# Seven block products of a SwiGLU pair in another order, in turn between two PSUM banks, and another tile for a pair's first weights

## The chip, the cores and the metric

The kernel runs on one core of one Trainium2 chip, in one launch. The metric is the device time of that core in microseconds, the median of several runs. Besides the runs there is one profiled execution with its own time.

## What is computed

Two layers of a decoder trunk on 256 positions of 1024 channels, in float32. Each layer is a half-step SwiGLU FFN, a token mixing, a second half-step SwiGLU FFN, each followed by a layer normalisation of the residual:

```python
def swiglu(x, wg, wu, wd):
    return (jax.nn.silu(x @ wg) * (x @ wu)) @ wd

def reference(x, ...):
    for l in range(DEPTH):                                   # DEPTH = 2
        x = layer_norm(ALPHA * x + 0.5 * swiglu(x, ffn_wg[l, 0], ffn_wu[l, 0], ffn_wd[l, 0]), ln_g[l, 0], ln_b[l, 0])
        m = token_mix(x, w_in[l], w_out[l], ...)
        x = layer_norm(ALPHA * x + m, ln_g[l, 1], ln_b[l, 1])
        x = layer_norm(ALPHA * x + 0.5 * swiglu(x, ffn_wg[l, 1], ffn_wu[l, 1], ffn_wd[l, 1]), ln_g[l, 2], ln_b[l, 2])
    return x
```

The FFN has 2816 hidden channels: `wg` and `wu` are 1024 x 2816, `wd` is 2816 x 1024. The token mixing (sparse attention, a pooling mixer, a gated linear attention, one input and one output projection) is not touched by the change.

## The kernel before

**Three matmuls for one.** The 256 positions are two tiles of 128 (t = 0, 1). A float32 product is made of three matmuls on values split in a high and a low part: high x high, high x low, low x high. ScalarE writes the high part of a weight block (`ACT.activation`, L232, L240, L260, L178: 128 x 1024 in about 1.05 us), VectorE the rest (`tensor_sub`, L233, L241, L262, L179: about 1.2 us for 1024 columns, 2.3 us for 2048). One *unit* of weights is two raw loads of 512 KB on SyncE's queue, split into one high tile `wh` and one low tile `wl` of 128 x 2048; there are four of each, and a unit's pair of tiles comes free when TensorE is done with it.

**Chunks and pairs.** The hidden channels are 11 chunks of 256. Chunks 0, 1 and 10 are computed plainly (`glu`, quarters of a chunk as units; `a10` and `b10` in the plan are the halves of chunk 10). Chunks 2 to 9 go in four pairs (2,3), (4,5), (6,7), (8,9), each by a Strassen-like scheme (Winograd's form) over two position tiles, two halves of the 1024 channels and the two chunks: seven block products in place of eight. `product` (L453) issues the 12 matmuls of one, of 512 columns each, at L462. Four of the seven use sums of the two position tiles (`make_sums`, named `sa` and `sb` in the trace), three use `xh`, `xl` themselves.

**Seven's weights** (`seven`, L134). Product 1 takes block 11 as it is; 5 takes 11 + 12; 6 takes 11 + 12 + 22; 4 takes 11 + 12 + 22 + 21 as the signs of the stored blocks make it; 7 takes 12 + 22, which a DMA on GpSimd's queue adds in place (L157); 3 takes 22, 2 takes 21. The running sum is built in the tile `fa`, into which block 11 is loaded (L142); VectorE adds 12, then 22 (L147), then 21 (L171), and each sum is split. `fa` shares its memory with the attention's keys, `fb` (block 12) with a weight of the mixing, `fc` (22) with a transposed tile of the attention. Block 21 goes into two of the four `raw` buffers that all plain units use.

**Banks.** Each pair holds two of four PSUM banks (named `g` and `tr` in the trace): `b1` and `b5`. Products 1, 6, 7 and 4 add up in `b1`; 5, and then 3 and 2, in `b5`:

```python
self.product(b1 if x in "1674" else b5, left[x], x in "15")
```

After a product its bank is copied out by ScalarE (`copy`, L476): 1 gives `c11`, 5 gives `cv`, 6, 7 and 3 the partial results of the second chunk. After 3 the copy `c11` is written into `b5` (L517) for product 2 to add to. `gated` (L527) applies SiLU and the product with the other half, on ScalarE and VectorE. The results are transposed by `h_T` (T in the plan) and split, and `down` (d in the plan, a unit of 24 matmuls, 12 for each position tile) multiplies them with `wd` into four banks `acc`.

**Order.** TensorE's order in this stage is written out by hand in `PLAN` and kept as written; S2, S4, S6, S8 open a pair. The units of weights are made in the same order, three units ahead of the one in use (`ahead`, L566). The other engines and queues are ordered by a scheduler that knows priorities: the copies and gates have a high one, but each engine works through its queue in order.

**Normalisation.** `ln_params` (L373) loads the 1024 scales and 1024 offsets to all 128 partitions, in two tiles, on GpSimd's queue, for the first normalisation on SyncE's; `layer_norm` (L385) uses them on VectorE (L400, L402) at the end of each of the six sub-layers.

Of the kernel before, what the change touches and what calls it, by code (L numbers as in the profile page):

```python
# [10 lines left out]
def _warn_once_fixed(msg, *args, **kwargs):  # L11
# [7 lines left out]
F32 = mybir.dt.float32  # L19
# [3 lines left out]
AF = mybir.ActivationFunctionType  # L23
# [4 lines left out]
D = 1024  # L28
# [9 lines left out]

PLAN = ("S2 1 T0 5 a10 6 b10 7 d0 3 4 2 S4 1 T2 d1 5 6 7 d2 3 4 2 S6 d3 1 T4 5 6 7 d4 3 4 2 "
        "S8 d5 1 T6 5 6 7 d6 T10 3 4 2 d7 T8").split()

LAST = (10, 8, 9)
WARM = ((7, 512), (4, 128))
# [11 lines left out]
def build(ctx, tc, d):  # L57
    nc = tc.nc
    PE, ACT, DVE, POOL = nc.tensor, nc.scalar, nc.vector, nc.gpsimd

    cst = ctx.enter_context(tc.tile_pool(name="cst", bufs=1))
    wp = ctx.enter_context(tc.tile_pool(name="wp", bufs=1))
    act = ctx.enter_context(tc.tile_pool(name="act", bufs=1))
# [53 lines left out]
    for t in range(2):  # L117
        vbd.append(cst.tile([128, 2, 2, 64], F32, name=f"vbd{t}"))
        a = cst.tile([128, 4, 128], F32, name=f"at{t}")
# [11 lines left out]
    def gate_up(l, f, c, q):  # L131
        return [d["wgu"][l, f, c, 2 * q + h] for h in range(2)]

    def seven(l, f, c):  # L134


        b = {}

        def load(to, c, q, pool, name, tag):
            b[to] = pool.tile([128, 2048], F32, name=name, tag=tag, bufs=1)  # L140
            for h, a in enumerate(gate_up(l, f, c, q)):
                last_dma[0] = nc.sync.dma_start(out=b[to][:, h * 1024:(h + 1) * 1024], in_=a)  # L142

        def add(x):
            for h in range(2):
                s = slice(h * 1024, (h + 1) * 1024)
                DVE.tensor_add(out=b["11"][:, s], in0=b["11"][:, s], in1=x[:, s])  # L147

        def f1():
            load("11", c, 0, cst, "fa", "ks")  # L150
            return split_wide(b["11"])

        def f5():
            load("12", c + 1, 0, cst, "fb", "s_w1")
            add(b["12"])
            for h, a in enumerate(gate_up(l, f, c + 1, 1)):
                nc.gpsimd.dma_start(out=b["12"][:, h * 1024:(h + 1) * 1024], in_=a, accum_op=ALU.add)  # L157
            return split_both(b["11"])

        def f6():  # L160
            load("22", c + 1, 1, mix, "fc", "pT")
            add(b["22"])
            return split_both(b["11"])

        def f4():
            b["21"] = []
            for h, a in enumerate(gate_up(l, f, c, 1)):
                raw = wp.tile([128, 1024], F32, name="raw", bufs=4)
                last_dma[0] = nc.sync.dma_start(out=raw, in_=a)
                s = slice(h * 1024, (h + 1) * 1024)  # L170
                DVE.tensor_add(out=b["11"][:, s], in0=b["11"][:, s], in1=raw)  # L171
                b["21"].append(raw)
            return split_both(b["11"])

        def f2():
            u = split_tiles()
            for raw, (wh, wl) in zip(b["21"], u):
                ACT.activation(out=wh, in_=raw, func=AF.Copy)  # L178
                DVE.tensor_sub(out=wl, in0=raw, in1=wh.bitcast(F32))  # L179
            return u  # L180

        return {"1": f1, "5": f5, "6": f6, "7": lambda: split_wide(b["12"]), "3": lambda: split_wide(b["22"]),
                "4": f4, "2": f2}

# [32 lines left out]
    last_dma = [None]  # L217
# [7 lines left out]
    def split_tiles():  # L225
        return in_halves(wide_tiles())
# [9 lines left out]
    def split_both(raw):  # L236
        u = split_tiles()
        for h, (wh, wl) in enumerate(u):
            s = slice(h * 1024, (h + 1) * 1024)
            ACT.activation(out=wh, in_=raw[:, s], func=AF.Copy)  # L240
            DVE.tensor_sub(out=wl, in0=raw[:, s], in1=wh.bitcast(F32))  # L241
        return u
# [109 lines left out]
    def make_sums(sums):  # L352

        s1, a11, a12, a21 = sums["s"], sums[0, 0], sums[0, 1], sums[1, 0]
        big = wp.tile([128, 2, 2, 4, 128], F32R, name="sb", tag="fb", bufs=1)

        def parts(f, i):
            tl = (mix.tile([128, 2, 4, 128], F32R, name=f"sa{i}", tag=("qs0", "qs1")[i], bufs=1) if i < 2
                  else big[:, i - 2])
            split(tl[:, 0], tl[:, 1], f.rearrange("p (a b) -> p a b", a=4))  # L360
            return tl[:, 0], tl[:, 1]
        first = parts(s1, 0)
        DVE.scalar_tensor_tensor(out=s1, in0=s1, scalar=-1.0, in1=a11, op0=ALU.mult, op1=ALU.subtract)
        DVE.tensor_sub(out=a21, in0=a11, in1=a21)
        DVE.scalar_tensor_tensor(out=a12, in0=a12, scalar=-1.0, in1=s1, op0=ALU.mult, op1=ALU.subtract)
        yield first
        yield parts(s1, 1)
        yield parts(a21, 2)
        yield parts(a12, 3)

    lnp = {}

    def ln_params(l, i):  # L373
        if (l, i) not in lnp:
            r = []
            for nm in ("ln_g", "ln_b"):
                tl = act.tile([128, D], F32, name="lnp_" + nm)
                src = d[nm][l, i]
                src = bass.AP(tensor=src.tensor, offset=src.offset, ap=[[0, 128], [1, D]])
                (nc.gpsimd if l + i else nc.sync).dma_start(out=tl, in_=src)  # L380
                r.append(tl)
            lnp[l, i] = r
        return lnp[l, i]

    def layer_norm(t, accs, l, i):  # L385
# [22 lines left out]
    class Ffn:  # L408
# [56 lines left out]
        def plan(self):  # L465
            a = [[tuple(p[:, 4 * q:4 * q + 4] for p in XT[t]) for q in range(2)] for t in range(2)]
            left = {"1": a[0][0], "2": a[0][1], "4": a[1][1]}
            sums = make_sums(self.sums)

            def f32():  # L470
                self.cc += 1
                return mix.tile([128, 512], F32, name="cc", tag=("vblk", "cc", "c40", "at011", "c41")[self.cc % 5], bufs=1)

            def copy(b, tag=None):
                r = mix.tile([128, 512], F32, name=tag, tag=tag, bufs=1) if tag else f32()
                ACT.activation(out=r, in_=b, func=AF.Copy)  # L476
                return r
            ahead_sums = [next(sums)]
            for x in PLAN:
                if x[0] == "S":  # L480
                    c = int(x[1:])

                    (w1, b1), (w5, b5) = self.bank(), self.bank()
                    if not m0 and c == 8:
                        with tc.issue_after(last_dma[0].ins):
                            late_constants()
                            m0.append(Mix(0))
                            ln_params(0, 0)
                elif x[0] in "abTd":
                    for t in range(2):  # L490
                        if x[0] == "T":
                            self.h_T(t, int(x[1:]) // 2)
                        elif x[0] == "d":
                            self.down(t, int(x[1:]))
                        else:
                            self.glu(t, int(x[1:]), "ab".index(x[0]))
                    continue
                else:
                    if x in "5673" and x not in left:
                        left[x] = ahead_sums.pop()  # L500
                        if x != "3":
                            ahead_sums.append(next(sums))
                    self.product(b1 if x in "1674" else b5, left[x], x in "15")
                with tc.high_priority():
                    if x == "1":
                        c11 = copy(b1)
                    elif x == "5":
                        v = copy(b5, "cv")
                    elif x == "6":
                        u = copy(b1)  # L510
                    elif x == "7":
                        c22 = copy(b1)
                        DVE.tensor_add(out=c22, in0=v, in1=c22)
                        self.gated(1, c + 1, c22, sign=-1.0)
                    elif x == "3":
                        w = copy(b5, "cw")
                        ACT.activation(out=b5, in_=c11, func=AF.Copy)  # L517
                        DVE.tensor_add(out=u, in0=w, in1=u)
                        self.gated(0, c + 1, u, sign=-1.0)
                    elif x == "2":  # L520
                        self.gated(0, c, b5, c11)
                        self.free.append(w5)
                    elif x == "4":
                        self.gated(1, c, b1, f32())
                        self.free.append(w1)
# [549 lines left out]
    for l in range(L):  # L1075
# [3 lines left out]
        out = [wout(m, t) for t in range(2)]  # L1079
# [104 lines left out]
```

## Time and profile before

| | |
|---|---|
| median of 3 runs | 1001.22 us (995.27 to 1007.08) |
| profiled execution, its own time | 999.5 us |
| its span, first to last instruction | 997.7 us |
| TensorE, matmuls / weight loads busy | 954.4 us (96%) / 773.8 us (78%) |
| VectorE, ScalarE, GpSimd busy | 850.5 us (85%), 637.6 us (64%), 56.3 us (6%) |
| HBM read | 193.68 MB, 195 GB/s over the span |
| mean granted clock of TensorE | 0.980 |

How to read the profile: a row of the timeline gives the start and the duration in us, the engine (PE is TensorE, DVE VectorE, ACT ScalarE, POOL GpSimd, SP SyncE; a "q" behind it is the engine's queue of issues), the source line, the operation, output<-inputs, shape, how many in a row, and in brackets how long the engine was idle before and what it waited for. Matmuls overlap: one of 512 columns is shown with a duration of 0.39 us, but the next may start earlier, so starts tell more than durations. A list of waits gives who waited for whom, us in total, how many times, and the longest. A table of windows gives for each stretch its length, the busy time and the count of each engine's instructions, the granted clock of TensorE, the DMA engines' share and GB/s.

### The profile page before, as it was taken

What the parts mean: (1) busy time and instruction counts of PE and PEld (TensorE: products, weight loads), DVE (VectorE), ACT (ScalarE), POOL (GpSimd) and SP (SyncE); (2) the same over time, 40 slices, a digit from 0 to 9 for tenths busy, and PEclk for the clock granted to TensorE, in tenths of its full rate; (3) what the DMA queues carried; (4) which work ended last, traced back from release to release, by engine and by line L of the source; (5) the groups of instructions that cost most, each with busy time, mean ns of one, the idle gap of its engine ahead of it and who ended that gap; (6) DMA issues with size and microseconds to landing.
All of it is one profiled execution on the core that took longest, in us unless ns stands there. A gap on an engine that the chain in (4) does not pass through costs nothing.

```text
span 997.7 us, 12731 instructions
## 1 busy us (share of the span) xinstructions
PE 954.4 (96%) x4579; PEld 773.8 (78%) x4579; DVE 850.5 (85%) x1194; ACT 637.6 (64%) x993; POOL 56.3 (6%) x82
## 2 busy tenths in 40 slices
PE   9989998999999999998999999899999999999997
PEld 6867786888778887877888877688887788877785
DVE  6978987787978979989799899887889699899884
ACT  6847657475675766667567667664677467677660
POOL 0000000010101000000000000001000010000000
PEclk9999998999999999999999999989999999999989
DMA  9856685665545575765857766565635366775551
GB/s 329 247 204 182 180 274 188 215 211 177 174 128 179 164 254 158 221 253 165 300 169 216 206 252 188 150 230 178 222 120 149 130 204 191 223 258 171 170 169 43
DMA packets 56480, 195.57 MB, mean 196 GB/s; under 512 B 7137, under 2 KB 8161, under 8 KB 56161
## 3 DMA queue, kind: packets, MB, share of 16 engines
q1 hardware_dynamic: 49824, 171.16, 49.9%
q0 software_dynamic: 6448, 23.53, 11.8%
q8 instruction: 36, 0.59, 0.2%
q14 instruction: 28, 0.22, 0.1%
q10 hardware_dynamic: 144, 0.07, 0.0%
HBM read 193.68 MB, written 1.05 MB: 195 GB/s over the span
## 4 chain that ended last, share of the span: by engine, by line
PE 56%; DVE 20%; ACT 8%; DMA 8%; issue 6%; POOL 0%; SPq 0%; DVEq 0%; POOLq 0%; ACTq 0%
PE acc L296 9%; PE acc L294 9%; PE acc L295 9%; PE tr L462 8%; DMA fa<-in_wgu 5%; PE g L462 5%; DVE wl L241 4%; DVE fa L147 4%; DVE wl L233 4%; ACT wh L232 3%; DMA fb<-in_wgu 2%; DVE wl L262 2%; PE tr L330 2%; ACT wh L260 2%; PE g L295 2%
## 5 line engine op out<-in xcount | busy, mean ns | idle before, releaser
L260 ACT ACTIVATE wh<-raw 128x1024 fp32r<-128x1024 f32 (+2 forms) x194 | 196.4, 1033 | 93.5 <-PE acc L296 44.6
L262 DVE TENSOR_TENSOR wl<-raw,wh 128x1024 fp32r<-128x1024 f32 (+2 forms) x194 | 226.3, 1188 | 20.3 <-ACT wh L260 19.8
L294 PE MATMUL acc<-wh,hi 128*128 128x512 f32 x352 | 138.5, 393 | 0.0
L295 PE MATMUL acc<-wl,hi 128*128 128x512 f32 x352 | 137.6, 391 | 0.0
L296 PE MATMUL acc<-wh,lo 128*128 128x512 f32 x352 | 137.3, 390 | 0.0
L240 ACT ACTIVATE wh<-fa 128x1024 fp32r<-128x1024 f32 x96 | 100.5, 1061 | 53.2 <-DVE fa L147 52.0
L241 DVE TENSOR_TENSOR wl<-fa,wh 128x1024 fp32r<-128x1024 f32 x96 | 115.7, 1221 | 2.1 <-ACT wh L240 1.6
L294 PEld LDWEIGHTS acc<-wh,hi 128*128 128x128 f32 x352 | 66.6, 189 | 13.6
L296 PEld LDWEIGHTS acc<-wh,lo 128*128 128x128 f32 x352 | 66.2, 188 | 14.0
L295 PEld LDWEIGHTS acc<-wl,hi 128*128 128x128 f32 x352 | 66.4, 189 | 13.6
L294 PE MATMUL acc<-wh,xh 128*128 128x512 f32 x192 | 76.3, 397 | 0.5 <-ACT xh L307 0.3
L296 PE MATMUL acc<-wh,xl 128*128 128x512 f32 x192 | 76.3, 397 | 0.0
L295 PE MATMUL acc<-wl,xh 128*128 128x512 f32 x192 | 76.0, 396 | 0.2 <-DVE wl L262 0.2
L462 PE MATMUL tr<-wh,sb 128*128 128x512 f32 x128 | 50.4, 459 | 14.3 <-ACT cc L476 14.3
L157 POOL DMA_DIRECT2D fb<-in_wgu x32 | 27.8, 870 | 492.3 <-DVE fa L147 300.9
L233 DVE TENSOR_TENSOR wl<-fa,wh 128x2048 fp32r<-128x2048 f32 x16 | 36.7, 2292 | 20.8 <-ACT wh L232 19.1
L462 PE MATMUL g<-wh,sb 128*128 128x512 f32 x128 | 43.6, 402 | 7.4 <-ACT cc L476 7.4
L462 PEld LDWEIGHTS tr<-wh,sb 128*128 128x128 f32 x128 | 28.5, 223 | 23.8 <-ACT cc L476 17.7
L232 ACT ACTIVATE wh<-fa 128x1024 fp32r<-128x1024 f32 x32 | 33.3, 1054 | 16.0 <-DMA fa<-in_wgu 10.4
L462 PE MATMUL g<-wh,sa 128*128 128x512 f32 x128 | 42.1, 395 | 0.0
L296 PEld LDWEIGHTS acc<-wh,xl 128*128 128x128 f32 x192 | 36.2, 188 | 7.6 <-DVE xl L308 0.6
L462 PE MATMUL tr<-wl,xh 128*128 128x512 f32 x96 | 38.5, 401 | 3.8 <-DVE wl L233 3.8
(288 smaller groups left out, 2191.9 us busy)
## 6 DMA issues: line engine op xcount, KB each, us to landing
raw<-in_wd SPq DMA_DIRECT2D x88, 512.0 KB, 5.1
raw<-in_wgu SPq DMA_DIRECT2D x79, 512.0 KB, 4.5
fa<-in_wgu SPq DMA_DIRECT2D x32, 512.0 KB, 5.1
fb<-in_wgu SPq DMA_DIRECT2D x32, 512.0 KB, 5.6
fc<-in_wgu SPq DMA_DIRECT2D x32, 512.0 KB, 5.7
fb<-in_wgu POOLq DMA_DIRECT2D x32, 512.0 KB, 6.8
raw<-in_win SPq DMA_DIRECT2D x32, 512.0 KB, 4.2
raw<-in_wout SPq DMA_DIRECT2D x16, 512.0 KB, 4.2
```

The source lines that it names most:

```text
L147: DVE.tensor_add(out=b["11"][:, s], in0=b["11"][:, s], in1=x[:, s])
L157: nc.gpsimd.dma_start(out=b["12"][:, h * 1024:(h + 1) * 1024], in_=a, accum_op=ALU.add)
L232: ACT.activation(out=wh[:, s], in_=raw[:, s], func=AF.Copy)
L233: DVE.tensor_sub(out=wl, in0=raw, in1=wh.bitcast(F32))
L240: ACT.activation(out=wh, in_=raw[:, s], func=AF.Copy)
L241: DVE.tensor_sub(out=wl, in0=raw[:, s], in1=wh.bitcast(F32))
L260: ACT.activation(out=wh[:, s], in_=raw[:, s], func=AF.Copy)
L262: DVE.tensor_sub(out=wl[:, s], in0=raw[:, s], in1=wh[:, s].bitcast(F32))
L294: pe(PE.matmul(ps, xh, wh, start=start, stop=False, skip_group_check=seeded))
L295: pe(PE.matmul(ps, xh, wl, start=False, stop=False, skip_group_check=seeded))
L296: pe(PE.matmul(ps, xl, wh, start=False, stop=stop, skip_group_check=seeded))
L462: pe(PE.matmul(ps, a[:, k, :], w[:, s], start=first and k == 0 and n == 0, stop=k == 3 and n == 2, skip_group_check=True))
```

## The change

The order of products in `PLAN` becomes 1 5 6 3 7 2 4, so that `b1` and `b5` follow each other in turn; the down units stand in other gaps between them. 2 now loads block 21 and 4 adds it later; `make_sums` gives its last two sums in the other order. Block 11 is loaded into a tile `fd` that shares its memory (tag `lnp`) with the normalisation's parameters, now one tile of 2 x 1024; 5's add reads `fd` and writes the running sum into `fa`. The parameters of the first normalisation are loaded on GpSimd's queue like the others.

```diff
-PLAN = ("S2 1 T0 5 a10 6 b10 7 d0 3 4 2 S4 1 T2 d1 5 6 7 d2 3 4 2 S6 d3 1 T4 5 6 7 d4 3 4 2 "
-        "S8 d5 1 T6 5 6 7 d6 T10 3 4 2 d7 T8").split()
+PLAN = ("S2 1 T0 5 a10 6 3 b10 7 2 d0 4 S4 1 T2 5 d1 6 3 d2 7 2 4 S6 d3 1 T4 5 6 d4 3 7 2 4 "
+        "S8 d5 1 T6 5 6 d6 3 T10 7 2 4 d7 T8").split()
...
-        def add(x):
+        def add(x, y=None):
             for h in range(2):
                 s = slice(h * 1024, (h + 1) * 1024)
-                DVE.tensor_add(out=b["11"][:, s], in0=b["11"][:, s], in1=x[:, s])
+                DVE.tensor_add(out=b["s"][:, s], in0=(b["s"] if y is None else y)[:, s], in1=x[:, s])
 
         def f1():
-            load("11", c, 0, cst, "fa", "ks")
+            load("11", c, 0, act, "fd", "lnp")
             return split_wide(b["11"])
 
         def f5():
             load("12", c + 1, 0, cst, "fb", "s_w1")
-            add(b["12"])
+            b["s"] = cst.tile([128, 2048], F32, name="fa", tag="ks")
+            add(b["12"], b["11"])
             for h, a in enumerate(gate_up(l, f, c + 1, 1)):
                 nc.gpsimd.dma_start(out=b["12"][:, h * 1024:(h + 1) * 1024], in_=a, accum_op=ALU.add)
-            return split_both(b["11"])
+            return split_both(b["s"])
 
         def f6():
             load("22", c + 1, 1, mix, "fc", "pT")
             add(b["22"])
-            return split_both(b["11"])
-
-        def f4():
+            return split_both(b["s"])
+
+        def f2():
             b["21"] = []
-            for h, a in enumerate(gate_up(l, f, c, 1)):
+            u = split_tiles()
+            for a, (wh, wl) in zip(gate_up(l, f, c, 1), u):
                 raw = wp.tile([128, 1024], F32, name="raw", bufs=4)
                 last_dma[0] = nc.sync.dma_start(out=raw, in_=a)
-                s = slice(h * 1024, (h + 1) * 1024)
-                DVE.tensor_add(out=b["11"][:, s], in0=b["11"][:, s], in1=raw)
-                b["21"].append(raw)
-            return split_both(b["11"])
-
-        def f2():
-            u = split_tiles()
-            for raw, (wh, wl) in zip(b["21"], u):
                 ACT.activation(out=wh, in_=raw, func=AF.Copy)
                 DVE.tensor_sub(out=wl, in0=raw, in1=wh.bitcast(F32))
+                b["21"].append(raw)
             return u
+
+        def f4():
+            for h, raw in enumerate(b["21"]):
+                s = slice(h * 1024, (h + 1) * 1024)
+                DVE.tensor_add(out=b["s"][:, s], in0=b["s"][:, s], in1=raw)
+            return split_both(b["s"])
...
-        yield parts(a21, 2)
-        yield parts(a12, 3)
+        yield parts(a12, 2)
+        yield parts(a21, 3)
...
-            r = []
-            for nm in ("ln_g", "ln_b"):
-                tl = act.tile([128, D], F32, name="lnp_" + nm)
+            tl = act.tile([128, 2, D], F32, name="lnp")
+            for n, nm in enumerate(("ln_g", "ln_b")):
                 src = d[nm][l, i]
                 src = bass.AP(tensor=src.tensor, offset=src.offset, ap=[[0, 128], [1, D]])
-                (nc.gpsimd if l + i else nc.sync).dma_start(out=tl, in_=src)
-                r.append(tl)
-            lnp[l, i] = r
+                nc.gpsimd.dma_start(out=tl[:, n], in_=src)
+            lnp[l, i] = [tl[:, 0], tl[:, 1]]
...
                     if x in "5673" and x not in left:
                         left[x] = ahead_sums.pop()
-                        if x != "3":
+                        if x != "7":
                             ahead_sums.append(next(sums))
```

## The prediction

> **What bounds the kernel now.** I read the page's busy times first, then the waits of TensorE, then the timeline around the longest of those waits, last the windows that show work and clock by stretch.
>
> ```profile
> PE 954.4 (96%) x4579; PEld 773.8 (78%) x4579; DVE 850.5 (85%) x1194; ACT 637.6 (64%) x993; POOL 56.3 (6%) x82
> ```
>
> TensorE is busy all the time and VectorE almost. What the first can still gain is in the list of its waits (who waited, for whom: us in total, times, longest):
>
> ```profile
> PE tr L462 <- ACT cc L476: 14.3, 8, 4.4
> PE tr L462 <- DVE wl L233: 7.9, 4, 3.8
> PE g L462 <- ACT cc L476: 7.4, 4, 2.0
> PE tr L462 <- DVE wl L241: 1.5, 2, 0.7
> ...
> PE g L462 <- DVE wl L233: 0.5, 1, 0.5
> ```
>
> All of these are at L462, the block products. 21.7 us in 12 waits (14.3 + 7.4) are waits for the copy of a bank by ScalarE (L476); 9.9 us are waits for weights that VectorE has not split yet (7.9 + 1.5 + 0.5). The 12 fall on the three later pairs of each of the four FFNs, every time between products 6 and 7; the first pair has a plain quarter (b10) there. The timeline of TensorE and ScalarE at one of them:
>
> ```profile
> 577.94 0.39 PE L462 MATMUL tr<-wh,sa 128*128 128x512 f32 x1
> 580.31 0.50 PE L462 MATMUL tr<-wh,sb 128*128 128x512 f32 x1 [1.98 <-ACT cc L476]
> ...
> 577.78 1.99 ACT L232 ACTIVATE wh<-fc 128x1024 fp32r<-128x1024 f32 x2
> 579.68 0.58 ACT L476 ACTIVATE cc<-tr 128x512 f32<-128x512 f32 x1
> ```
>
> Product 6 issues its last matmul at 577.94. Product 7 adds into the same bank, so the copy must read it first; the copy stands behind two splits of 1.99 us, and product 7 starts 2.37 us after that matmul.
>
> The pace without waits comes from these rows:
>
> ```profile
> 583.18 0.39 PE L294 MATMUL acc<-wh,hi 128*128 128x512 f32 x1
> ...
> 588.62 0.39 PE L462 MATMUL tr<-wh,sb 128*128 128x512 f32 x1
> ...
> 596.78 0.39 PE L294 MATMUL acc<-wh,hi 128*128 128x512 f32 x1
> ```
>
> From 583.18 to 588.62 run the 24 matmuls of one down unit: 5.44 us, 0.227 us each. From 588.62 to 596.78 run products 3, 4 and 2: 36 matmuls at 0.227 too, so a product is 2.72 us, and the two changes of bank among them cost nothing. Two windows that follow waits, first and last of seven, and one whole pair (columns: TensorE, its weight loads, VectorE, ScalarE, GpSimd; then granted clock):
>
> ```profile
> 66.00:78.00 12.00, 8.25 (x29) 6.41 (x28) 6.98 (x7) 5.46 (x10) 0.86 (x1) 0.72 0.39 116
> 944.00:957.00 13.00, 10.50 (x33) 7.83 (x32) 11.32 (x10) 9.78 (x12) 0.00 (x0) 0.74 0.27 83
> 880.00:913.00 33.00, 31.14 (x140) 25.53 (x140) 30.94 (x30) 22.14 (x30) 1.71 (x2) 1.00 0.71 223
> ```
>
> 0.28 x 12 and 0.26 x 13 are 3.4 us lost to a lower clock each. Of the seven stretches four lose 3.4 and three 1.7 us: 18.7 us. Waits and clock together put 31.6 + 18.7 = 50.3 us, 5% of the time, within reach; the matmuls themselves stay.
>
> **The change, part by part.** *Order and banks.* After 6 now comes 3 (or a down unit, then 3), in the other bank. So from the last matmul of 6 to the first of 7 there are at least 0.23 + 2.72 = 2.95 us, against 2.37 above: the copy fits with 0.6 us to spare, and with 5.44 us more in every pair, because a down unit or b10 also stands there. The 12 waits go, 21.7 us, but for the longest. That one, in the last pair of the first FFN, has another cause:
>
> ```profile
> 158.64 1.22 DVE L171 TENSOR_TENSOR fa<-fa,raw 128x1024 f32<-128x1024 f32 x1 [3.32 <-DMA raw<-in_wgu]
> 161.38 0.80 PE L462 MATMUL tr<-wh,sb 128*128 128x512 f32 x1 [4.36 <-ACT cc L476]
> ```
>
> VectorE waited for a raw block that the constants of the token mixing had held up in the DMA queue, and ScalarE's copy behind it. That load keeps its place (seventh unit of its pair, now issued for 2), so I leave 4.4 us and its 3.4 us of clock standing, and count 17.3 us.
>
> *New links.* 2 must now wait for the copy of 3 and for the seed (L517) with only 7 between in the last two pairs, 4 for the copy of 7 with only 2 between in the last three. Before, 3 and 2 stood apart by product 4, as far:
>
> ```profile
> 591.54 0.60 ACT L476 ACTIVATE cw<-tr 128x512 f32<-128x512 f32 x1 [0.66 <-PE tr L462]
> ...
> 592.98 0.59 ACT L517 ACTIVATE tr<-cc 128x512 f32<-128x512 f32 x1
> ```
>
> Product 3 began at 588.62, so 2 wants the bank at 588.62 + 2 x 2.72 = 594.06; the seed is there at 593.57. 0.5 us to spare, with a split between the two, and no wait of TensorE on it in the list. A copy alone needs 0.6 us less. ScalarE will idle less, so I charge 0.5 us to each of the 12 later pairs, 6 us, between nothing and the 2.2 us that such a link cost before.
>
> *The buffer.* Today the first block of the next pair goes into the tile that holds the running sum, and can be loaded only when the last split of 4 has read it. Last pair of the third FFN, SyncE's queue, ScalarE, VectorE and TensorE:
>
> ```profile
> 622.23 0.80 SPq L142 DMA_DIRECT2D fa<-in_wgu  x2
> ...
> 628.77 1.06 ACT L232 ACTIVATE wh<-fa 128x1024 fp32r<-128x1024 f32 x1 [2.14 <-DMA fa<-in_wgu]
> ...
> 630.13 0.42 DVE L531 SCALAR_TENSOR_TENSOR cc<-cc,g 128x256 f32<-128x256 f32 x1 [3.05 <-ACT cc L530]
> 631.10 2.29 DVE L233 TENSOR_TENSOR wl<-fa,wh 128x2048 fp32r<-128x2048 f32 x1 [0.55 <-ACT wh L232]
> ...
> 645.32 0.39 PE L462 MATMUL tr<-wh,sa 128*128 128x512 f32 x1
> ...
> 648.78 0.80 PE L462 MATMUL tr<-wl,sb 128*128 128x512 f32 x1 [1.31 <-DVE wl L233]
> ```
>
> VectorE loses 3.05 + 0.55 = 3.6 us behind the late load, works without a pause after it, and product 7 gets its weights at 648.78 instead of 645.55: 3.2 us late, and the clock falls. With a tile of its own the load waits only for the add of 5, some 20 us earlier (the add ran from 597.79 in the pair before, below, the load went out at 622.23); the 3.6 us come back and the lateness is gone. The 3.8 us wait of the second pair in the first FFN (the longest on L233) starts in the same way. I count 9.4 of the 9.9 us of weight waits, and 18.7 - 3.4 = 15.3 us of clock.
>
> How short a wait costs clock is seen in a window and the only wait in it:
>
> ```profile
> 391.00:399.00 8.00, 6.09 (x21) 4.52 (x20) 6.65 (x5) 4.25 (x7) 0.00 (x0) 0.79 0.68 226
> ...
> 393.83 0.50 PE L462 MATMUL tr<-wh,sb 128*128 128x512 f32 x1 [1.91 <-ACT cc L476]
> ```
>
> 1.91 us idle, and the clock is granted at 0.79 of 8 us. [...]
>
> *VectorE's share.* The same adds and splits are made, in another order: no term. But the pair above has 30.94 us of VectorE work in 33.00 us, and TensorE without its wait of about 2 us needs 31: the two are level, and VectorE's turn decides. A unit without an add (594.89), units with one, by their starts, and product 1 on TensorE:
>
> ```profile
> 594.89 2.29 DVE L233 TENSOR_TENSOR wl<-fa,wh 128x2048 fp32r<-128x2048 f32 x1 [0.53 <-ACT wh L232]
> ...
> 597.79 2.35 DVE L147 TENSOR_TENSOR fa<-fa,fb 128x1024 f32<-128x1024 f32 x2
> 600.14 2.36 DVE L241 TENSOR_TENSOR wl<-fa,wh 128x1024 fp32r<-128x1024 f32 x2
> 602.42 2.36 DVE L147 TENSOR_TENSOR fa<-fa,fc 128x1024 f32<-128x1024 f32 x2
> ...
> 602.22 0.39 PE L462 MATMUL g<-wh,xh 128*128 128x512 f32 x1
> ```
>
> 4.6 us for a unit with adds (5, 6, 4), 2.3 without, against 2.72 us of a product and 5.44 of a down unit. In the new second pair (1 5 d 6 3 d 7 2 4) two down units stand between the heavy ones, and by the same addition, unit for unit, the weights stay 1 to 5 us ahead. In the third and fourth pair 5 and 6 still stand together: 4.6 + 4.6 + 1.1 for the first half of the down unit are 10.3 us against 3 x 2.72 = 8.2, so 2.1 us of the lead that product 1 brings (5.0 us in this pair: weights at 597.18, product at 602.22) are used; it is not overdrawn.
>
> *Normalisation.* Its parameters now share the tile with that first block. They are loaded on GpSimd's queue behind the accumulating loads of the last pair, after the add of 5; five products and five down units, 40.8 us, are then to come on TensorE before they are used. A load takes about 5 us (row below): hidden, with 35 us to spare. The other way round, the first block of an FFN waits for the normalisation:
>
> ```profile
> 509.33 1.41 DVE L402 SCALAR_TENSOR_TENSOR x<-x,ve,lnp_ln_b 128x512 f32<-128x512 f32 x2
> ...
> 516.96 1.99 ACT L232 ACTIVATE wh<-fa 128x1024 fp32r<-128x1024 f32 x2
> ...
> 527.38 0.39 PE L462 MATMUL g<-wh,xh 128*128 128x512 f32 x1
> ...
> fa<-in_wgu SPq DMA_DIRECT2D x32, 512.0 KB, 5.1
> ```
>
> Free at 510.7, landed 5.1 to 7.5 us later, the split may begin at 518 instead of 516.96. Its product comes at 527.38: hidden by 6 us, three times; nothing. What SyncE has queued behind it is for later units, so nobody else waits earlier. The two loads moved to GpSimd are 0.4 us of issue each, nothing either.
>
> **Sum**: 17.3 + 9.4 + 15.3 - 6 = 36.0 us. The profiled execution took 999.5 us (span 997.7 and 1.8 outside), 1.7 below the median of 1001.22; 999.5 - 36 = 963.5, and I give 965 for a median.
>
> **Rivals.** *VectorE becomes the bound.* For: 30.94 of 33 us, and it stands still behind ScalarE in its own queue, in rows that no order of products removes:
>
> ```profile
> DVE cc L531 <- ACT cc L530: 17.7, 18, 3.0
> DVE cc L513 <- ACT cc L476: 6.6, 7, 1.5
> ```
>
> 24.3 us over 16 pairs are 1.5 us; a pair then takes 30.9 + 1.5 = 32.4 us. Today two pairs take 645.32 - 577.94 = 67.4, 33.7 each: 1.3 us saved on 12 pairs, 16 us, with more or less of the clock 12 to 24: 976 to 988. Against: these waits fall where VectorE is ahead and are shorter when it is late. *The wait only moves*, to weights or to another copy: 990 to 1010. The load in the first FFN shows how a copy's wait can hide a late weight.
>
> *The copies come late at the new links*, the case on the other side. Its price is in this row, a split that holds up ScalarE until VectorE has added:
>
> ```profile
> 603.67 1.06 ACT L240 ACTIVATE wh<-fa 128x1024 fp32r<-128x1024 f32 x1 [2.43 <-DVE fa L147]
> ```
>
> If such a split of 4 stands ahead of a copy, the seed is 2.43 - 0.5 = 1.9 us late (8 times) and the copy of 7 about 1.5 us (12 times), each with 1.7 us of clock: 33 + 34 = 67 us against 42 of gain, about 1025. It decides from 42 / 20 = 2.1 us a link, clock included. Against: 3, 4, 2 had the same distance and no wait.
>
> *Alternating banks itself slows TensorE.* More changes of bank, six a pair instead of five, each ending in a cold stretch of 1.7 us, would take 16 x 1.7 = 27 us off the gain: about 990. The 36 matmuls above at 0.227 us across two changes speak against it. [...]
>
> **Chances.** The forecast (949 to 976) 0.58; VectorE as the bound 0.22; the wait only moves 0.10, alternating banks 0.03; late copies 0.07. The range runs from 949 (all 50.3 us) to 991, where the moved wait and the late copies begin and 0.17 to 0.2 is left out. Within 1% is about what a measurement of this kernel cannot tell from no change. Faster by more: 0.58 + 0.22 = 0.80; within: 0.13; slower: 0.07.
>
> **What would show it.** Right: the 12 waits on L476 between 6 and the next product gone; no wait of ScalarE on the first block's load but at the head of an FFN; granted clock 1.0 through the second to fourth pair; such a pair in about 31.5 us. Wrong: waits of L462 on L517 or L476 ahead of products 2 or 4; waits on wl in the third and fourth pair with VectorE busy throughout; a normalisation that waits for its parameters.

## The result, and the profile after

The changed kernel takes 952.17 us (median of 4 runs, 951.43 to 953.06); the kernel before took 1001.12 us beside it (4 runs, 995.27 to 1007.08). The ratio is 0.951, interval 0.945 to 0.957. The forecast was 965, the range 949 to 991; the gain is 49 us where 36 were summed. The profiled execution took 953.06 us with a span of 951.3 us, 46.4 less than before; the mean granted clock rose from 0.980 to 0.999. In three later groups of runs, 29 in all, the kernel before took 996.56 us (median, 992.35 to 1001.38), so the four runs above put it somewhat high: against those the gain is 44 to 45 us, a ratio of 0.954 to 0.956. In one of these groups one run of the changed kernel took 1338.27 us at a granted clock of 0.654; the ratios leave it out.

The page's busy times and the whole list of TensorE's waits, after (who waited for whom: us in total, times, longest; L461 are the block products, L475 the copy of a bank, L516 the seed for product 2, one line earlier than before):

```profile
PE 934.7 (98%) x4579; PEld 764.2 (80%) x4579; DVE 844.1 (89%) x1194; ACT 634.1 (67%) x993; POOL 57.4 (6%) x84
```

```profile
PE tr L461 <- DVE wl L242: 2.2, 1, 2.2
PE tr L541 <- DVE hh L447: 1.6, 2, 1.1
PE acc L106 <- DVE zw L109: 1.2, 1, 1.2
PE tr L331 <- ACT pT L900: 1.1, 2, 0.6
PE tr L652 <- DVE gaT L650: 0.9, 2, 0.5
PE tr L331 <- DVE sq L961: 0.6, 2, 0.3
PE tr L461 <- DVE wl L234: 0.5, 1, 0.5
PE g L541 <- DVE cc L530: 0.3, 1, 0.3
PE acc L295 <- ACT xh L308: 0.3, 1, 0.3
PE acc L296 <- DVE wl L263: 0.2, 1, 0.2
```

All 12 waits on the copy are gone, also the one of the first FFN that the prediction had left standing. At the block products 2.7 us are left of 31.6. New are the 1.9 us at L541 (transposes of the gated values); the other rows stood there before.

The balance closes from these two views alone. Waits at the products: 31.6 - 2.7 = 28.9 us won. New waits: -1.9, and 0.2 for a row that went. Clock: 0.020 x 997.7 = 20.0 us lost before, 0.001 x 951.3 = 1.0 now, 19.0 won. Together 46.2, and the spans differ by 46.4. That they agree so closely is partly chance: some 5 us of the waits of before lie in stretches at half clock, so about 2.6 us stand in both terms, and a wait costs about 0.3 us more than its row says (same_bank_7_4, below). The busy times give the same in another split: 954.4 - 934.7 = 19.7 us less of TensorE's busy time for the same 4579 matmuls, and 26.7 less of idle.

One later pair in the windows (length; TensorE, its weight loads, VectorE, ScalarE, GpSimd; granted clock, DMA share, GB/s), then the end of such a pair on all engines, after:

```profile
867.30:898.10 30.80, 30.80 (x141) 25.60 (x140) 29.47 (x29) 21.59 (x29) 2.82 (x4) 1.00 0.78 237
```

```profile
568.59 0.82 SPq L142 DMA_DIRECT2D fd<-in_wgu  x2
...
588.92 0.39 PE L461 MATMUL g<-wh,sb 128*128 128x512 f32 x1
...
591.84 0.60 ACT L475 ACTIVATE cw<-g 128x512 f32<-128x512 f32 x1 [0.66 <-PE g L461]
...
593.28 0.59 ACT L516 ACTIVATE g<-cc 128x512 f32<-128x512 f32 x1
...
594.36 0.39 PE L461 MATMUL g<-wh,xh 128*128 128x512 f32 x1
...
595.06 0.59 ACT L475 ACTIVATE cc<-g 128x512 f32<-128x512 f32 x1
...
595.53 2.00 ACT L233 ACTIVATE wh<-fd 128x1024 fp32r<-128x1024 f32 x2
```

A pair lasts 30.8 us with TensorE busy throughout, against the 33.00 us window of a pair before; 31.5 were forecast. Product 3 runs from 588.92, 7 behind it, 2 from 594.36, 5.44 us later, at 0.227 us a matmul across the changes of bank. The seed of 2 is written by 593.87, 0.49 us early: the half microsecond to spare that the prediction had worked out, and it is enough. The copy of 7 ends at 595.65, 1.4 us before product 4 begins at 597.08. The next pair's first block was ordered at 568.59 and is split at 595.53, 27 us later; before, 6.5 us lay between the two (622.23 and 628.77).

The first FFN's last pair, where the prediction had left a wait of 4.36 us standing. Before, VectorE, SyncE's queue and ScalarE; then ScalarE's first split of 7's weights (`fb`) after:

```profile
131.81 1.22 DVE L241 TENSOR_TENSOR wl<-fa,wh 128x1024 fp32r<-128x1024 f32 x1
...
133.09 0.80 SPq L142 DMA_DIRECT2D fa<-in_wgu  x2
...
157.90 1.06 ACT L232 ACTIVATE wh<-fb 128x1024 fp32r<-128x1024 f32 x1 [2.23 <-DMA fb<-in_wgu]
...
160.75 0.57 ACT L476 ACTIVATE cc<-tr 128x512 f32<-128x512 f32 x1
```

```profile
147.16 1.07 ACT L233 ACTIVATE wh<-fb 128x1024 fp32r<-128x1024 f32 x1
```

Before, the load into `fa` went out at 133.09, when the last split of 4 had read the tile (131.81 + 1.22). SyncE's queue had issued nothing for 4.1 us; 13 loads of constants and parameters, four of weights and the raw block for 4 stood behind it, the last 4 MB of them ordered from 140.08 to 143.97. The accumulating load that turns `fb` into 7's weights was ordered behind all these, at 144.80 and 145.70. From 146 to 158 the DMA engines are busy throughout (share 1.03, 312 GB/s), and it landed at 157.88, 12.2 us after the second order, against a median of 6.8. ScalarE waited 2.23 us for it, then did that split and two of a down unit, and copied product 6 at 160.75: that is the wait of 4.36 us. The prediction had put it down to the raw block that VectorE waited for in these same microseconds. No instruction of ScalarE ahead of the copy waited for that block; the two late loads came out of one jam. After, the load into `fd` goes out at 104.77, the constants follow each other from 121.61, the accumulating loads are ordered at 132.83 and 136.26 and land by 144.62, and the split of `fb` at 147.16 waits for nothing.

What the change cost, VectorE's and ScalarE's waits on the new tile, after, and ScalarE's on the old one, before:

```profile
DVE fa L147 <- DMA fd<-in_wgu: 7.0, 3, 3.0
...
ACT wh L233 <- DMA fd<-in_wgu: 2.7, 3, 2.3
```

```profile
ACT wh L232 <- DMA fa<-in_wgu: 10.4, 8, 2.8
```

Three waits of VectorE, at the heads of the FFNs behind a normalisation, where the prediction said "hidden by 6 us".

### The profile page after: what moved, and what is told of

The parts are those of the page before. It is cut to its first block, busy times and chain, and to the rows that moved or that the text cites. A ratio compares the mean times of both kernels' runs of the same rounds, so it can differ in the third digit from the quotient of the medians.

```text
span 951.3 us, 12752 instructions
## 1 busy us (share of the span) xinstructions
PE 934.7 (98%) x4579; PEld 764.2 (80%) x4579; DVE 844.1 (89%) x1194; ACT 634.1 (67%) x993; POOL 57.4 (6%) x84
## 4 chain that ended last, share of the span: by engine, by line
PE 73%; DVE 13%; ACT 5%; DMA 4%; issue 3%; POOL 0%; DVEq 0%; SPq 0%; ACTq 0%
PE tr L461 15%; PE g L461 13%; PE acc L297 10%; PE acc L295 10%; PE acc L296 10%; DVE wl L263 3%; DMA fd<-in_wgu 3%; ACT wh L261 2%; DVE wl L234 2%; PE tr L331 2%; PE g L296 2%; DVE fa L147 2%; PE g L295 2%; PE g L297 1%; PE acc L322 1%
## 5 line engine op out<-in xcount | busy, mean ns | idle before, releaser
L241 ACT ACTIVATE wh<-fa 128x1024 fp32r<-128x1024 f32 x96 | 99.6, 1056 | 73.1 <-DVE fa L147 48.2
L242 DVE TENSOR_TENSOR wl<-fa,wh 128x1024 fp32r<-128x1024 f32 x96 | 115.8, 1219 | 6.0 <-ACT wh L241 5.6
L147 DVE TENSOR_TENSOR fa<-fd,fb 128x1024 f32<-128x1024 f32 x32 | 38.6, 1218 | 7.1 <-DMA fd<-in_wgu 7.0
L461 PE MATMUL tr<-wh,sb 128*128 128x512 f32 x128 | 42.5, 393 | 0.0
L461 PE MATMUL g<-wh,sa 128*128 128x512 f32 x128 | 42.1, 395 | 0.0
L461 PE MATMUL tr<-wh,sa 128*128 128x512 f32 x128 | 42.1, 395 | 0.0
L295 PEld LDWEIGHTS acc<-wh,xh 128*128 128x128 f32 x192 | 36.2, 189 | 7.3 <-ACT xh L308 0.5
L296 PEld LDWEIGHTS acc<-wl,xh 128*128 128x128 f32 x192 | 36.3, 189 | 7.1 <-DVE wl L263 0.5
L233 ACT ACTIVATE wh<-fb 128x1024 fp32r<-128x1024 f32 x32 | 32.4, 1058 | 13.9 <-PE tr L297 7.0
```

The source lines that it names most:

```text
L147: DVE.tensor_add(out=b["s"][:, s], in0=(b["s"] if y is None else y)[:, s], in1=x[:, s])
L233: ACT.activation(out=wh[:, s], in_=raw[:, s], func=AF.Copy)
L295: pe(PE.matmul(ps, xh, wh, start=start, stop=False, skip_group_check=seeded))
L296: pe(PE.matmul(ps, xh, wl, start=False, stop=False, skip_group_check=seeded))
L461: pe(PE.matmul(ps, a[:, k, :], w[:, s], start=first and k == 0 and n == 0, stop=k == 3 and n == 2, skip_group_check=True))
```

## The experiments

The theory was that the two parts remove two independent losses, the order the waits for the copy and the tile those for weights, and that the clock follows. The first rival: the parts aren't independent, and the waits removed by one come back under the other's name. The second: the alternation of banks is what counts, not the time between two products of one bank. The third: VectorE is the bound, and the rest moves only inside its slack. A table of all versions stands behind the runs.

**order_only**: the new plan and banks, block 11 still loaded into `fa` and summed in place, the parameters' tiles as before.

```diff
 (against the changed kernel)
-            load("11", c, 0, act, "fd", "lnp")
+            load("11", c, 0, cst, "fa", "ks")
...
-            b["s"] = cst.tile([128, 2048], F32, name="fa", tag="ks")
+            b["s"] = b["11"]
```

> The new order and the new use of the banks, but block 11 is loaded into the tile of the running sum as before, and the normalisation's parameters keep their own tiles. Theory: the order removes the 12 waits on L476 between 6 and 7 (21.7 us and most of the 15 us of clock), the late reload of the first block stays: VectorE still loses about 3.6 us behind it in a pair, and as TensorE now comes earlier, waits on wl appear in several pairs. So about 25 to 33 of the 49 us are gained: 968 to 976 us, with ScalarE waiting for the DMA of fa again. Rival, the buffer is of no weight: 952 us, no waits on wl. Rival, the buffer does nearly all: over 990 us.

996.72 us (10 runs, 992.63 to 1000.1), ratio 1.000 [0.997, 1.003], clock 0.986. A miss for the theory: the order alone gives nothing. The first of TensorE's waits, and ScalarE's on the first block:

```profile
PE tr L463 <- DVE wl L242: 9.9, 10, 1.9
PE g L463 <- DVE wl L242: 6.8, 5, 1.8
PE tr L463 <- DVE wl L234: 3.8, 4, 2.8
PE g L463 <- ACT wh L241: 3.2, 4, 1.8
PE tr L463 <- ACT wh L241: 2.7, 4, 1.6
PE tr L463 <- ACT wh L233: 2.4, 1, 2.4
```

```profile
ACT wh L233 <- DMA fa<-in_wgu: 35.2, 17, 6.9
```

No copy (L477 in this kernel) is in the list, but 29.6 us of waits for weights are (28.8 in the rows shown, 0.8 in two more); before, both kinds made 31.6. ScalarE's wait for the reload has grown from 10.4 to 35.2 us. One end of a pair shows why (VectorE's last split of 4, the reload, the splits of the block's second half, TensorE):

```profile
585.16 1.22 DVE L242 TENSOR_TENSOR wl<-fa,wh 128x1024 fp32r<-128x1024 f32 x1
586.40 0.80 SPq L142 DMA_DIRECT2D fa<-in_wgu  x2
...
593.35 1.06 ACT L233 ACTIVATE wh<-fa 128x1024 fp32r<-128x1024 f32 x1 [1.72 <-DMA fa<-in_wgu]
...
594.45 2.29 DVE L234 TENSOR_TENSOR wl<-fa,wh 128x2048 fp32r<-128x2048 f32 x1 [2.36 <-ACT wh L233]
...
596.79 0.50 PE L463 MATMUL g<-wl,xh 128*128 128x512 f32 x1 [0.51 <-DVE wl L234]
```

From the last reader of `fa` (586.38) to product 1's low weights (596.74) are 10.4 us. VectorE stands idle for some 5 of them: 2.36 in the row above, and 2.50 at 591.66 ahead of a gate whose part on ScalarE stands behind the reloaded block's first split. 4 is now the last product of its pair. By the order of the units, in the last two pairs 2 and a down unit were split in this time before and now the down unit alone, in the second pair 2 before and now nothing: 2.3 us of VectorE's work less to cover the reload. This last step is read from the plan; cover_no_tile, below, bears on it.

**buffer_only**: the order and banks of before, with the tile `fd` and the shared parameters.

```diff
 (against the kernel before)
-            load("11", c, 0, cst, "fa", "ks")
+            load("11", c, 0, act, "fd", "lnp")
...
+            b["s"] = cst.tile([128, 2048], F32, name="fa", tag="ks")
+            add(b["12"], b["11"])
...
+            tl = act.tile([128, 2, D], F32, name="lnp")
```

> The old order and banks, with the new tile for block 11 shared with the normalisation's parameters. Theory: the 12 waits between 6 and 7 stay (21.7 us, 2 us each, little clock), the waits on wl (9.9 us) and the clock that they cost go: 10 to 20 us gained, 981 to 991 us. Rival, the order is all: 1001 us. Rival, the buffer is nearly all: under 965 us, the wait between 6 and 7 shortened as well.

971.46 us (970.81 to 973.64), ratio 0.976 [0.972, 0.980], clock 0.992. More than expected. The weight waits are gone and the 12 waits on the copy stand:

```profile
PE tr L461 <- ACT cc L475: 8.8, 8, 3.9
PE g L461 <- ACT cc L475: 6.2, 4, 4.1
```

Ten of the 12 are now of 0.69 us, for instance here, where ScalarE was idle and copied at once (timeline of ScalarE, 2.15 us idle, waiting for product 6):

```profile
602.77 0.60 ACT L475 ACTIVATE cc<-g 128x512 f32<-128x512 f32 x1 [2.15 <-PE g L461]
```

So 0.7 us of idle time is what two products of one bank behind each other cost when ScalarE is free, about 1 us in all (worked out at same_bank_7_4); the 2 us of before were mostly ScalarE's backlog after a late reload. The two long waits are in the first FFN. In both ScalarE had itself waited for the accumulated block in `fb` (1.76 us at 81.24, 2.73 us at 118.40), with the copy behind it, so they say little of the bank. Around these two the clock falls:

```profile
79.00:92.00 13.00, 8.84 (x26) 6.40 (x26) 8.08 (x5) 7.56 (x10) 0.00 (x0) 0.75 0.50 162
118.00:131.00 13.00, 8.90 (x28) 6.79 (x27) 8.48 (x6) 7.97 (x10) 0.00 (x0) 0.74 0.59 194
```

**same_bank_7_4**: the changed kernel with 4 ahead of 2, so that 7 and 4, of one bank, follow each other 12 times; block 21 is loaded for 4 again.

```diff
-PLAN = ("S2 1 T0 5 a10 6 3 b10 7 2 d0 4 S4 1 T2 5 d1 6 3 d2 7 2 4 S6 d3 1 T4 5 6 d4 3 7 2 4 "
-        "S8 d5 1 T6 5 6 d6 3 T10 7 2 4 d7 T8").split()
+PLAN = ("S2 1 T0 5 a10 6 3 b10 7 d0 4 2 S4 1 T2 5 d1 6 3 d2 7 4 2 S6 d3 1 T4 5 6 d4 3 7 4 2 "
+        "S8 d5 1 T6 5 6 d6 3 T10 7 4 2 d7 T8").split()
```

> The changed kernel, but 4 before 2 in each pair, so that 4 follows 7 in the same bank (with a down unit between them in the first pair of an FFN); block 21 is again loaded for 4. Theory, a product next to another in its bank waits for the copy: 12 waits of about 2 us on L476 come back, now ahead of 4, and in some pairs a stretch of low clock: 24 to 45 us more than 952, 976 to 997 us. Rival, the gain came from where the down units stand and from the buffer: 952 us, within 5.

965.54 us (963.95 to 966.48), ratio 0.969 [0.966, 0.973], clock 0.999: 13.4 us more than the changed kernel, and 10 us less than the low end of what was expected.

```profile
PE tr L461 <- ACT cc L475: 7.7, 8, 1.2
PE g L461 <- ACT cc L475: 4.7, 4, 1.2
```

The 12 waits come back as the theory says, 12.4 us, but of 1.2 us at most and with no loss of clock. Their price was taken from before, where it held the backlog and the clock too. The waits at the products grew by 10.5 us (12.4 for copies and 0.8 for weights, against 2.7), the span by 13.4, since a wait costs more than its row. At a row of 0.69 us, TensorE's last matmul of 7 starts at 569.16 and the first of 4 at 570.23, 1.07 us later where 0.227 would do, and the twelve of 4 take 0.13 us longer than at full pace: 0.98 us. Twelve times the 0.29 us between the two are 3.5 us, which makes up the difference.

**add_of_5_twice**: the changed kernel with the add of 5 made twice, to the same values: 2.3 us more of VectorE in each of 16 pairs.

```diff
             add(b["12"], b["11"])
+            add(b["12"], b["11"])
```

> The changed kernel with the add of product 5 made twice, the same values: 2.3 us more VectorE work in each of the 16 pairs, nothing else. Theory, VectorE and TensorE are level (30.9 against 31 us) in the three later pairs: each of these 12 gets about 2 us longer, 972 to 980 us, with waits on wl. Rival, TensorE alone is the bound and VectorE has room: 952 to 957 us.

975.32 us (971.91 to 978.55), ratio 0.979 [0.974, 0.984]: as expected. Its busy times, and the largest of the waits that came:

```profile
PE 941.3 (97%) x4579; PEld 764.9 (79%) x4579; DVE 880.1 (91%) x1226; ACT 634.1 (65%) x993; POOL 57.3 (6%) x84
```

```profile
PE tr L462 <- DVE wl L243: 10.8, 9, 2.8
```

VectorE has 36 us more to do (880.1 - 844.1). The four runs lie in two groups, at 972 and at 978.5; in the profiled one (971.91) the span grows by 18.8 us, of which the clock, 0.995, takes some 4. So 17 to 21 us were absorbed there, and 13 by the median: about 1 us a pair, and the rest passes through. VectorE isn't the bound of the changed kernel, but it is only about that far from it.

**order_no_reload**: order_only again, but block 11 is loaded for the first pair of an FFN alone and later pairs split what the tile holds. That leaves out 12 loads of 1 MB, and those products are of other values.

```diff
 (against order_only)
-            load("11", c, 0, cst, "fa", "ks")
+            if c == 2:
+                load("11", c, 0, cst, "fa", "ks")
+                kept[0] = b["11"]
+            b["11"] = kept[0]
```

> The new order with the sum built in place, as in the run with the order alone, but block 11 is loaded for the first pair of an FFN only; later pairs split what the tile holds, so the products' values are not the reference's. Theory, what the order loses without the new tile is the latency of the reload (about 6.5 us after the last split of 4): 950 to 958 us, the waits on wl nearly gone. Rival, the tile itself is the tie, or VectorE's work in this order: 975 us or more. Rival, DMA traffic: some 2 us of either.

949.05 us (948.13 to 949.78), ratio 0.953 [0.951, 0.956], clock 0.999. Without the reload the order alone gives everything. It also takes 12 MB off the DMA queues, which this run can't tell apart from the wait; the changed kernel does load them, and comes within 3 us. The parameters have their old tiles here, so it isn't their new place that gains.

**old_order_cover**: buffer_only with the old order of products and the old banks, and a down unit put between 6 and 7 in each later pair (in the second pair one is taken from ahead of 5).

```diff
-PLAN = ("S2 1 T0 5 a10 6 b10 7 d0 3 4 2 S4 1 T2 d1 5 6 7 d2 3 4 2 S6 d3 1 T4 5 6 7 d4 3 4 2 "
-        "S8 d5 1 T6 5 6 7 d6 T10 3 4 2 d7 T8").split()
+PLAN = ("S2 1 T0 5 a10 6 b10 7 d0 3 4 2 S4 1 T2 5 6 d1 7 d2 3 4 2 S6 d3 1 T4 5 6 d4 7 3 4 2 "
+        "S8 d5 1 T6 5 6 d6 7 T10 3 4 2 d7 T8").split()
```

> The old order 1 5 6 7 3 4 2 and the old banks with the new tile, but a down unit between 6 and 7 in the three later pairs. Theory, what counts is that something covers the copy, and that the load is early: 950 to 955 us, as the changed kernel, the 12 waits on L475 gone. Rival, the banks in turn are needed: 960 to 971 us.

949.30 us (947.83 to 951.21), ratio 0.954 [0.951, 0.956]. The block products wait once, for 0.8 us (on L242). Alternating banks isn't needed: a down unit, which adds into other banks, does it between 6 and 7 as well.

**cover_no_tile**: the same plan in the kernel before, without the new tile.

> The kernel before (old order, old banks, block 11 in the tile of the running sum) with a down unit between 6 and 7 in the three later pairs. Theory, the order alone gained nothing because it puts 4 last, one split (2.3 us) ahead of the next pair's first, which leaves the reload of 6.5 us more in the open; here 2 and a down unit stand between as before (4.6 us), so the 12 copy waits go and part of the gain remains: 970 to 988 us, with some waits on wl. Rival, cover is worth nothing without the tile, wherever 4 stands: 993 to 1000 us. Rival, the late 4 was the whole trouble: 950 to 955 us.

976.06 us (975.21 to 977.65), ratio 0.978 [0.976, 0.981], as expected. What waits, and ScalarE's wait for the reload:

```profile
PE tr L462 <- DVE wl L241: 7.9, 8, 1.9
PE tr L462 <- DVE wl L233: 2.7, 1, 2.7
PE g L462 <- DVE wl L241: 2.6, 3, 0.9
```

```profile
ACT wh L232 <- DMA fa<-in_wgu: 19.8, 13, 4.3
```

No copy, 13.2 us of waits for low weights; the wait for the reload stands between that of before (10.4) and of order_only (35.2). Where 2 still follows 4, less of the gain is lost.

**head_in_place** and **cover_head**: the changed kernel, and old_order_cover, with the first pair of each FFN as before, so that only three of four pairs use `fd`.

```diff
-            load("11", c, 0, act, "fd", "lnp")
+            if c == 2:
+                load("11", c, 0, cst, "fa", "ks")
+                b["s"] = b["11"]
+            else:
+                load("11", c, 0, act, "fd", "lnp")
```

> The changed kernel, but the first pair of each FFN builds its sum in place, with block 11 loaded into fa as before, so that this load need not wait for the normalisation. Theory: the three waits of VectorE on that load (7.0 us) go and with them TensorE's waits at the first transposes (1.6 us and some clock at the start of a block): 949 to 951 us. Rival, the first pair's spare time hides the load wholly, as was forecast: 952 us, within 1.

> The old order with a down unit between 6 and 7, the new tile, and the first pair of each FFN in place: the two versions that were a little faster than the change, together. Theory: 949.3 less the 1 to 2 us that the first pair gave: 947 to 949 us. Rival, they overlap: 949 to 951 us.

head_in_place 950.65 us (949.33 to 951.43), ratio 0.955 [0.952, 0.957]; the changed kernel beside it 951.96. VectorE's three waits and the 1.6 us at L541 are gone, and the time is 1.3 us less, about what the runs scatter. cover_head is the best version: 948.36 us (947.6 to 948.99), ratio 0.950 [0.948, 0.952], below every run of the changed kernel beside it (951.2 to 953.1, median 952.63), though by 0.4% only.

**changed_again** and **changed_third**: the changed kernel itself, with the later groups of runs, as their yardstick.

> The changed kernel once more, as the measure for the three beside it: 951 to 954 us.

> The changed kernel beside it, as the measure: 951 to 953 us.

951.96 and 952.63 us, ratios 0.956 [0.954, 0.959] and 0.954 [0.952, 0.957].

The two changes side by side, as ratios to the kernel before:

| order | `fa` reloaded | tile `fd` |
|---|---|---|
| old | 1 | 0.976 |
| old, a down unit between 6 and 7 | 0.978 | 0.954 |
| new (1 5 6 3 7 2 4) | 1.000 | 0.951 to 0.956 |

The middle row is nearly a sum, 2.2 + 2.4 against 4.6%. The bottom row isn't: 0 and 2.4 against 4.4 to 4.9%.

## Why the prediction was right or wrong

Term by term, from the waits and clocks of the two traces:

| term of the sum | predicted, us | measured, us |
|---|---|---|
| waits for the copy | 17.3 | 21.7 |
| waits for weights | 9.4 | 7.2 |
| clock | 15.3 | 19.0 |
| new links | -6 | 0 |
| other new waits | 0 | -1.7 |
| sum | 36.0 | 46.2 |

*New links*: the mis-sized term. No wait on L516 or L475 is in the list, so the charge of 0.5 us a pair was nothing. The working (0.5 us to spare) came out as it was, 0.49 us; the charge came from "ScalarE will idle less", and though it does, 634.1 us busy in a span shorter by 46, it copies in time. That the backlogs behind the late reloads are gone is the likely reason; buffer_only, where ScalarE copies at once, speaks for it.

*The first FFN's last pair*: the reading failed ahead of the argument. The copy hung on the accumulated block in `fb`, not on the raw block. "That load keeps its place" failed too: its place in the order of units was kept, its place in time wasn't, because the load ahead of it in SyncE's queue was the held-up one. So a wait that the prediction gave to neither part belonged to the tile and the parameters' loads. 4.4 us, and some 3.4 of clock, went with them: in buffer_only already, no wait of 4 us stands in this pair (the two left, 3.9 and 4.1 us, are in the windows at 79 and 118).

These two, 6 + 4.4 + 3.7 of clock, less 2.2 of weight waits and 1.7 of new ones, are the 10.2 us between 36.0 and 46.2.

*Copy waits, as a mechanism*: right, with a flaw that the total hides. The prediction gave the order 17.3 us and the tile 9.4, as if each part could be had alone. The order alone gives 0, since it exposes more of the reload; the tile alone gives 24, since it also shortens ten copy waits to 0.69 us by clearing ScalarE's backlog. The step that failed is that the tile's part ended at VectorE's wait; the late reload reached TensorE by two ways, the weights and the copies queued behind the splits that came late. The sum held because both parts were made together, which is luck for a sum that priced them apart: the forecasts for one part alone missed, 968 to 976 for the order (996.72 measured) and 981 to 991 for the tile (971.46).

*Weights*: right in kind, 7.2 us for 9.4. ScalarE waits for the first block only at the head of an FFN (three waits), as the prediction asked. 2.7 us remain. The longest, 2.2 us at 83.11 in the first FFN's second pair, comes of another late load, the raw block for 4, which was ordered at 70.06 and which VectorE waited for with half of 6's split behind the add:

```profile
80.70 1.22 DVE L180 TENSOR_TENSOR fa<-fa,raw 128x1024 f32<-128x1024 f32 x1 [3.33 <-DMA raw<-in_wgu]
```

*Head of an FFN, "nothing"*: a small miss. The prediction followed the split and its product, not VectorE's queue, where the add of 5 reads the same tile and stands ahead of the position sums. After, at the head of the second FFN:

```profile
490.37 1.23 DVE L147 TENSOR_TENSOR fa<-fd,fb 128x1024 f32<-128x1024 f32 x1 [2.95 <-DMA fd<-in_wgu]
491.51 0.68 DVE L309 TENSOR_TENSOR sa<-s,sa 128x512 fp32r<-128x512 f32 x1
```

Three such waits make 7.0 us on VectorE; TensorE waits 1.6 us later on (L541), and head_in_place puts the price at about 1 us of time, within its scatter.

*Clock*: 3.7 us more than predicted, 3.4 of them the stretch that had been left standing with the first FFN's wait. That waits of 2 us were counted too, for the reason of the 0.79 after 1.91 us, was right. But length alone doesn't decide, since the wait of 1.98 us at 580.31 has the full clock (1.00 in the windows) before and after it. The trace of before shows where the two differ. Its granted clock is 0.50 from 70.24, 158.98, 647.09 and 947.46 for 6.83 us each, from 124.85, 394.50 and 462.77 for 3.41 us each, and from 995.25 to the end. All these changes lie on one grid with steps of 3.413 us: those at 124.85, 158.98, 394.50 and 647.09 come 16, 26, 95 and 169 steps behind the first one at 70.24, and each low stretch but that at the very end is one or two steps long. The two waits, cut along this grid (the columns as in the windows above):

```profile
391.09:394.50 3.41, 1.50 (x7) 0.95 (x6) 3.41 (x4) 3.41 (x5) 0.00 (x0) 1.00 0.42 127
394.50:397.91 3.41, 3.41 (x10) 2.64 (x9) 3.15 (x2) 0.23 (x1) 0.00 (x0) 0.50 0.83 274
...
575.41:578.82 3.41, 2.92 (x13) 2.06 (x11) 3.41 (x3) 3.41 (x6) 0.00 (x0) 1.00 0.00 0
578.82:582.23 3.41, 1.92 (x8) 1.61 (x9) 3.41 (x3) 2.39 (x4) 0.00 (x0) 1.00 0.90 277
```

The 1.91 us lie whole in one step, TensorE is busy for 1.50 of 3.41 us, and the next step has half the clock. The 1.98 us are cut by the edge at 578.82 into 0.49 and 1.49, and the clock stays. Without its first 8 and last 12 us this trace has 275 steps at full clock. The clock fell behind the five with 1.91 to 3.09 us of idle time, behind two of the four with 1.68 to 1.84 (those of 1.73 and 1.77), and behind none of the 266 with 1.52 or less. The changed kernel's wait of 2.24 us, from 80.87 to 83.11, cost no clock in its first profile, whose one fall, at 948.69, gives the grid an edge at 81.70: 0.83 us lie ahead of it, and TensorE is idle for 1.76 us of the step behind it. In the profile of changed_again, which has 2.3 us in the same row, the clock over the span is 0.996 against 0.999.

*Rivals*: alternating banks slowing TensorE is refuted (clock 0.999, 0.227 us a matmul). Late copies at the new links did not come. VectorE as the bound was near, by the 1 us a pair of add_of_5_twice. The wait that only moves is what order_only shows, and it came by a way that the prediction hadn't drawn: the new order makes the last reader of `fa` later, and the tile in the same change keeps that from mattering.

Open: what decides about the clock in steps with 1.68 to 1.84 us of idle time; how much of order_no_reload's time is the 12 MB that it doesn't load; and which part of the jam in the first FFN's last pair the tile took away and which the parameters' loads, now behind the accumulating ones (buffer_only has both).

## What to carry to other kernels

Before summing the gains of two edits to one loop, follow the same late event through both: a reload that holds up one engine shows up as waits on two others, and taking one of them away can lengthen the other by nearly the same amount (order_only: 29.6 us of waits for weights where both kinds had made 31.6). Here a load that waited for its buffer until 133.09 also held all that was queued behind it on SyncE for 4.1 us, so a row that waits for a DMA is read together with what stood ahead of that DMA in its queue. The cost of a wait in the trace is that of its queue as it was; measured without the backlog, in buffer_only and same_bank_7_4, the same copy cost 0.7 to 1.2 us of idle time instead of 2.

## What was not expected of the hardware

Twenty-two waits of 0.69 to 1.2 us (twelve in same_bank_7_4, ten in buffer_only) cost next to no clock: 0.999 over the whole of same_bank_7_4, and of the 7.8 us that buffer_only loses at 0.992, 6.6 lie in the 13 us at 0.75 and at 0.74 around its two waits of about 4 us. Between them lie the waits of 2 us of before, and there the two compared above differ by their place on a grid of 3.413 us: 1.91 us inside one step were followed by a step at half clock, 1.98 us cut in two by an edge by none. That fits the scatter in time of a kernel with such waits: the 29 later runs of the kernel before go from 992.35 us (clock 0.990) to 1001.38 us (0.980), those of the changed kernel in the groups from 951.2 to 953.1.
